# Modulations of two blocks side by side, norm sums in four column groups, modulations turned by transposes

## Chip, cores and metric

The kernel runs on one core of a Trainium2 chip. The metric is the device time of one execution in microseconds (us), lower is better; the time of a kernel is the median of several executions. The program computes in 32-bit floats, with nearly every large product split into a high and a low part.

## What is computed

One adaLN-modulated hybrid block (grouped-query attention beside a Fourier mixer) over 512 latent tokens of width 2048. The change touches only its first lines, and the head of the first projection:

```python
shift, scale, gate = jnp.split(silu_c @ w_ada[l] + b_ada[l], 3, axis=-1)
shift_c, scale_c, gate_c = jnp.split(silu_cc @ w_ada[l] + b_ada[l], 3, axis=-1)
h = _modulate(_rmsnorm(xs, norm_g[l]), shift[:, None], scale[:, None])   # h*(1+scale)+shift
p = h @ w_l            # attention, Fourier mixer, gates and output follow
```

The RMS norm needs the sum of squares of each token over all 2048 channels; the shift and the scale of each channel need a product of the vector `silu(c)` with 2048 rows of `w_ada`. Both must be there before the first block of 128 channels of `h` can enter a matmul.

## The kernel before, in words

Channels lie on the 128 partitions, so `xt` holds 16 blocks (`kb` 0 to 15) of 128 channels by 512 tokens. The part that the change touches is the start stage, about the first 150 us. It has three jobs on the matrix engine.

**Token norms** (`token_norms`, L513 to L536). ACT squares each block (L524, L528), DVE adds the squares of two blocks (L529, a 128x512 tile, 8 in all), and for each such tile one matmul with an all-ones stationary tile (L530) adds it over partitions into one PSUM bank, so that every partition has all 512 sums. Four ACT roots (L534) take 32 partitions each with the sums of 128 tokens, DVE takes the reciprocal (L535), and `spread` (L538) copies the result to all partitions through four matmuls (L541). The result scales every block.

**Modulations** (`modulate`, L559). For each block, `matvec` (L549) multiplies `c2` (32 columns, of which two are used: `c` and `c_ctx`) with 16 tiles of 128x256 of `w_ada`, on four groups of 32 columns of the array that work at the same time and write four groups of 32 PSUM rows (L553). ACT copies the result (`taken`, L569); `turned` (L571) multiplies it with `four`, a 0/1 matrix that adds the four groups and turns rows to columns in one step (L573, two matmuls with two columns each); DVE makes `gain` and `shift` of the block from them (L580, L582).

**Projection** (`start_work`, L638). As blocks of `h` come, they are multiplied with pieces of `w_in` of 1024 columns (L327 to L329 and L653 to L656): one step of `some(1)` is one 128x128 tile of the piece against 512 tokens, three matmuls (high by high, high by low, low by high), or, in pieces that pair two blocks in a private sum, six.

The order on PE is written by hand (`manual_schedule`), from L704 to L803: `modulate`, `columns` and `make_h` of each block stand between steps of the projection, so that the copy on ACT and the small DVE operations are covered by matmuls. From block six on, a loop (L766) takes one block after the other: three projection steps, the split of a weight piece on ACT and DVE (`split_next`, L176 and L177), `modulate`, one or two steps, `columns`, `make_h` (the high and low part of `h`, L611 to L614), and steps again. ACT and DVE have the same hand-written order up to block 13; for blocks 14 and 15 a scheduler orders them. The loads are issued by SP in the order of the program: for each block two loads of 1 MB of `w_ada` (`wada_load`, L481, tiles `wa`, four buffers, so the loads of a block wait until the block two before it has been multiplied) and one of 512 KB of `w_in` (`load_start`, tiles `wr`, four buffers).

After the start stage the rest of the program (Fourier mixer, the large projections, attention, output) follows; its order isn't touched.

Of the kernel before, what the change touches and what calls it, by code (L numbers as in the profile page):

```python
# [10 lines left out]
F32 = mybir.dt.float32  # L11
F32R = mybir.dt.float32r
ACT = mybir.ActivationFunctionType
ALU = mybir.AluOpType
# [105 lines left out]
def block_kernel(ctx, tc, xT, ctx_rows, ctx_toks, x, c_row, w_ss, w_gate, vecs, qkg, rope, dft_c, dft_s,  # L120
# [360 lines left out]
    def wada_load(kb):  # L481
        r = []
        for h in range(2):
            r.append(pap.tile([P, 8, 256], F32, tag="wada", bufs=4, name=uid("wa")))
            ask(nc.sync, r[-1], w_ss[kb, :, 8 * h : 8 * h + 8, :])
        return r

    for n in range(len(XCH)):
# [6 lines left out]

    c2 = pap.tile([P, KK, 32], F32, name="c2")
    nc.vector.memset(c2, 0.0)
    four = pap.tile([P, 2], F32, name="four")
    nc.vector.tensor_reduce(four, ident.rearrange("p (g r) -> p r g", g=4)[:, 0:2, :], axis=AX.X, op=ALU.add)
# [10 lines left out]
    fsq = [ppool.tile([P, 2, 2, T], F32R, name="fsq0")]  # L510
    rx = pap.tile([P, T], F32, name="rx")
    wacc = bank3()
    def token_norms():  # L513

        t = hm_tile([P, 2, T], F32, name=uid("nm"))
        pick, r = t[:, 0, :].rearrange("p (t c) -> p t c", t=4), t[:, 1, :P]
        nc.gpsimd.memset(pick, 0.0)
        for t in range(4):
            nc.gpsimd.memset(pick[32 * t : 32 * t + 1, t, :], 1.0)
        acc = bank2()  # L520
        for q in range(0, KK, 2):
            two = hm_tile([P, 2, T], F32, name=uid("sq"))
            a, b = two[:, 0, :], two[:, 1, :]
            nc.scalar.activation(a, xt[:, q, :], ACT.Square)  # L524
            if q in (6, 10):
                nc.vector.tensor_tensor(b, xt[:, q + 1, :], xt[:, q + 1, :], op=ALU.mult)
            else:
                nc.scalar.activation(b, xt[:, q + 1, :], ACT.Square)  # L528
            nc.vector.tensor_tensor(a, a, b, op=ALU.add)  # L529
            nc.tensor.matmul(acc, ones, a, start=q == 0, stop=q == KK - 2)  # L530

        for t in range(4):
            k = slice(32 * t, 32 * t + 32)
            nc.scalar.activation(r[k], acc[k, t * P : t * P + P], ACT.Sqrt, bias=eps_t[k, 0:1], scale=1.0 / D)  # L534
        nc.vector.reciprocal(r, r)  # L535
        return pick, r  # L536

    def spread(pick, r):  # L538
# [1 line left out]
        for t in range(4):  # L540
            nc.tensor.matmul(acc[:, t * P : t * P + P], pick[:, t, :], r, start=True, stop=True)  # L541
        return acc

    def warm(n, src):

        for _ in range(n):
            nc.tensor.matmul(wacc[:, :256], ones, src, start=True, stop=True)

    def matvec(kb, h):  # L549
        acc, w = two[kb][:, :256], wada[kb][h]  # L550
# [17 lines left out]
        wada.pop(kb)  # L568
        return nc.scalar.copy(o, two[kb][:, :256])  # L569

    def turned(sp, o):  # L571
        for i in range(2):
            nc.tensor.matmul(sp[:, 2 * i : 2 * i + 2], o[:, P * i : P * i + P], four, start=True, stop=True)  # L573

    def columns(kb):
        sp, o = two.pop(kb)[:, 256:], o_of.pop(kb)
        turned(sp, o)
        if kb == 0:
            warm(3, o)
        nc.vector.tensor_scalar(gain[:, kb, :], sp[:, 2:4], bsc1[:, kb : kb + 1], ng[:, kb : kb + 1],  # L580
                                op0=ALU.add, op1=ALU.mult)
        last = nc.vector.tensor_scalar(shift[:, kb, :], sp[:, 0:2], bada[:, kb : kb + 1], None, op0=ALU.add)  # L582
        return last

    rx0, y_of = [], {}
# [118 lines left out]
    with tc.manual_schedule(engines={E.PE}):  # L704
# [3 lines left out]
        rx0.append(spread(*norms))  # L708
        matvec(0, 1)
        with tc.manual_schedule(engines={E.Activation, E.DVE}):  # L710
            split_next()
            nc.scalar.copy(rx, rx0[0])
            by_root(0)
            taken(0)
            wada[2] = wada_load(2)
            load_start()
# [15 lines left out]
            some(2)  # L732
            for kb in range(1, 4):
                k = kb + 1
                some(2)
                by_root(k)
                modulate(k, split_next)
                if kb < 3:
                    wada[k + 2] = wada_load(k + 2)
                    load_start()  # L740
                hold()
                some(2)
                columns(k)
                row_hi(k)
                release()
# [20 lines left out]
            for kb in range(4, KK - 4, 2):  # L766
                some(3)
                split_next()
                for i in range(2):
                    k = kb + 2 + i  # L770
                    if i:
                        some(3)
                        split_next()
                    modulate(k)
                    if k + 2 < KK:
                        wada[k + 2] = wada_load(k + 2)
                        for _ in range(2 if k + 2 == KK - 3 else 1):
# [5 lines left out]
                    if k >= 8:  # L783
                        form_row(k - 8)
                some(1)
                if kb == KK - 6:
                    split_table(0)
                    split_from(get(("dftc", 0)), fch[:, 0, :], fch[:, 1, :])
                    load_start()
        for i in range(2):  # L790
            k = KK - 2 + i
            some(2)
            modulate(k)
            some(2 - i)
            columns(k)
            ins = make_h(k)
            with behind(ins):
                split_next()
                form_row(k - 8)
# [1166 lines left out]
```

## Time and profile before

| | |
|---|---|
| median of 3 runs | 1306.31 us (1306.24 to 1306.71) |
| the profiled execution | 1307.42 us |
| its span (first to last instruction) | 1305.7 us |
| PE busy | 1280.5 us, 98% of the span |
| DVE, ACT busy | 993.6 us, 687.5 us |
| the chain that ended last | PE 88%, DMA 4%, DVE 3%, ACT 2%, issue 2% |
| mean DMA rate over the first 140 us | 346 GB/s |

The profile is of one execution; times in it are us from the span's start. PE is the matrix engine, ACT the scalar engine, DVE the vector engine, SP the engine that issues most loads. A row of the timeline gives the start, the length, the engine, the source line, output<-inputs, the sizes, and how many instructions were merged into it. Matmuls are pipelined: what counts is the distance of the starts of two matmuls, not the length of one. A 32-bit matmul shows as two records ("passes"), so eight matmuls with c2 are 16 records.

### The profile page before, as it was taken

To read this page: it belongs to the slowest core of one execution; us is meant where nothing else is said; L and a number is where in the kernel's file an instruction comes from. 1 tells how busy PE (TensorE), PEld (TensorE's weight loads), DVE (VectorE), ACT (ScalarE), POOL (GpSimd) and SP (SyncE) were. 2 spreads that over 40 slices of the span, in tenths; PEclk is the share of its full clock that TensorE was granted. 3 is DMA by queue.
4 is the path that set the end of the run, shared out by engine and by line. 5 is a ranking of instruction groups with operands and counts; after the bars stand their busy time and mean duration, and the time that the engine had idled before them with its cause. 6 is when DMAs were issued, how large, how long until landed. Compare 5 with 4: busy or idle time off the path is not lost.

```text
span 1305.7 us, 17605 instructions
## 1 busy us (share of the span) xinstructions
PE 1280.5 (98%) x6554; PEld 1051.1 (81%) x6554; DVE 993.6 (76%) x1286; ACT 687.5 (53%) x1081; POOL 170.1 (13%) x220
## 2 busy tenths in 40 slices
PE   7999999999999999999999999999999999999997
PEld 3677888888888788888888888888888888888885
DVE  4656899979787787758677766688898767887676
ACT  5322655545556455444254554666667646464554
POOL 0000011110202111011021010011110212221210
PEclk9999999999999999999999999999999999999998
DMA  9988487888898889977869897467862899998985
GB/s 379 392 346 339 161 246 194 233 234 277 205 299 251 231 284 283 303 202 186 262 205 282 275 232 248 170 225 239 258 223 82 238 256 236 248 211 232 222 202 170
DMA packets 104053, 318.54 MB, mean 244 GB/s; under 512 B 9856, under 2 KB 33024, under 8 KB 99872
## 3 DMA queue, kind: packets, MB, share of 16 engines
q1 hardware_dynamic: 54912, 197.86, 41.7%
q0 software_dynamic: 26736, 97.14, 34.7%
q10 hardware_dynamic: 22320, 22.42, 5.0%
q8 instruction: 51, 0.84, 0.2%
q14 instruction: 34, 0.28, 0.1%
HBM read 283.30 MB, written 34.09 MB: 243 GB/s over the span
## 4 chain that ended last, share of the span: by engine, by line
PE 88%; DMA 4%; DVE 3%; ACT 2%; issue 2%; POOL 0%; SPq 0%; DVEq 0%; ACTq 0%; POOLq 0%
PE banks L327 9%; PE banks L328 9%; PE banks L329 9%; PE x L328 8%; PE x L329 8%; PE x L327 8%; PE y L329 7%; PE y L327 7%; PE y L328 7%; PE banks L1454 2%; PE pd L553 2%; DMA s<-yb_d 2%; PE pb L327 2%; PE pb L329 1%; PE pb L328 1%
## 5 line engine op out<-in xcount | busy, mean ns | idle before, releaser
L176 ACT ACTIVATE whi<-R 128x1024 fp32r<-128x1024 f32 x138 | 145.9, 1060 | 143.9 <-PE banks L329 49.2
L177 DVE TENSOR_TENSOR wlo<-R,whi 128x1024 fp32r<-128x1024 f32 x138 | 168.0, 1222 | 60.9 <-ACT whi L176 60.5
L177 DVE TENSOR_TENSOR wlo<-wr,whi 128x1024 fp32r<-128x1024 f32 (+1 forms) x122 | 147.3, 1213 | 61.2 <-ACT whi L176 60.9
L176 ACT ACTIVATE whi<-wr 128x1024 fp32r<-128x1024 f32 (+1 forms) x122 | 127.5, 1051 | 112.7 <-PE y L329 38.5
L327 PE MATMUL banks<-whi,s 128*128 128x512 f32 x396 | 157.0, 397 | 2.1 <-DVE ev L1021 1.5
L329 PE MATMUL banks<-whi,s 128*128 128x512 f32 x396 | 155.1, 392 | 0.0
L328 PE MATMUL banks<-wlo,s 128*128 128x512 f32 x396 | 155.0, 391 | 0.0
L328 PE MATMUL x<-wlo,s 128*128 128x512 f32 x356 | 138.7, 390 | 2.1 <-DVE wlo L177 2.1
L327 PE MATMUL x<-whi,s 128*128 128x512 f32 x356 | 138.8, 390 | 0.0
L329 PE MATMUL x<-whi,s 128*128 128x512 f32 x356 | 138.5, 389 | 0.0
L327 PE MATMUL y<-whi,s 128*128 128x512 f32 x308 | 120.1, 390 | 0.5 <-DVE cxe L1174 0.4
L329 PE MATMUL y<-whi,s 128*128 128x512 f32 x308 | 119.8, 389 | 0.5 <-DVE s L177 0.5
L328 PE MATMUL y<-wlo,s 128*128 128x512 f32 x308 | 119.9, 389 | 0.0
L280 POOL DMA_DIRECT2D R<-in_w_g x64 | 56.0, 874 | 415.9 <-DVE wlo L177 261.5
L176 ACT ACTIVATE s<-wr 128x512 fp32r<-128x512 f32 (+2 forms) x95 | 61.3, 677 | 66.8 <-DMA wr<-in_w_g 21.0
L177 DVE TENSOR_TENSOR s<-wr,s 128x512 fp32r<-128x512 f32 (+2 forms) x95 | 68.0, 749 | 27.6 <-ACT s L176 26.7
L327 PEld LDWEIGHTS banks<-whi,s 128*128 128x128 f32 x396 | 74.4, 188 | 17.6 <-ACT whi L176 1.9
L329 PEld LDWEIGHTS banks<-whi,s 128*128 128x128 f32 x396 | 74.4, 188 | 15.6
L328 PEld LDWEIGHTS banks<-wlo,s 128*128 128x128 f32 x396 | 74.4, 188 | 14.0 <-DVE wlo L177 0.2
L328 PEld LDWEIGHTS x<-wlo,s 128*128 128x128 f32 x356 | 66.8, 188 | 16.6 <-DVE wlo L177 2.9
L329 PEld LDWEIGHTS x<-whi,s 128*128 128x128 f32 x356 | 66.8, 188 | 13.9
L327 PEld LDWEIGHTS x<-whi,s 128*128 128x128 f32 x356 | 66.8, 188 | 13.7
(310 smaller groups left out, 2828.3 us busy)
## 6 DMA issues: line engine op xcount, KB each, us to landing
wr<-in_w_g SPq DMA_DIRECT2D x128, 512.0 KB, 5.4
wa<-in_w_ss SPq DMA_DIRECT2D x32, 1024.0 KB, 7.4
R<-in_w_g POOLq DMA_DIRECT2D x64, 512.0 KB, 7.3
R<-in_w_g SPq DMA_DIRECT2D x32, 512.0 KB, 5.9
wr<-in_w_gate SPq DMA_DIRECT2D x32, 512.0 KB, 4.8
wr<-in_w_o SPq DMA_DIRECT2D x24, 512.0 KB, 7.6
R<-in_w_o POOLq DMA_DIRECT2D x24, 512.0 KB, 8.8
wr<-in_w_pab SPq DMA_DIRECT2D x20, 512.0 KB, 6.1
```

The source lines that it names most:

```text
L176: first = nc.scalar.activation(hi, src, ACT.Copy)
L177: return first, nc.vector.tensor_tensor(lo, src, hi.bitcast(F32), op=ALU.subtract)
L280: nc.gpsimd.dma_start(chain[e.pc], e.nxt, accum_op=ALU.add)
L327: nc.tensor.matmul(o, ah, bh, start=start, stop=False, skip_group_check=cont)
L328: nc.tensor.matmul(o, ah, bl, start=False, stop=False, skip_group_check=cont)
L329: nc.tensor.matmul(o, al, bh, start=False, stop=stop, skip_group_check=cont)
L553: nc.tensor.matmul(acc[32 * j : 32 * j + 32], c2[:, n, :], w[:, k, :], start=n < 4, stop=n >= KK - 4)
L1454: nc.tensor.transpose(tp[:, k * P : (k + 1) * P], p[:, k * P : (k + 1) * P], ident)
```

## The change

Four edits, all in the start stage.

- **Norm sums.** Each pair tile of squares is now summed by four matmuls with 32 columns of ones each (L536): token group `t` of 128 tokens goes to PSUM rows `32t` to `32t+31`. So one ACT root over 128x128 takes the place of four (L540). Behind each of the first seven pairs two filler matmuls of 128x256 (`warm`, L516) are queued on PE, behind the last pair one; their output is not used.
- **Turned by transposes.** `turned` now transposes both halves of the copied result (L575, two transposes of 128x128), and `factors` adds the four groups by a DVE `tensor_reduce` (L586) before `gain` and `shift`.
- **Two blocks side by side.** From block six on, `modulate` of two blocks stands together, and so do their transposes; the projection steps between them are put elsewhere: eight ahead of the pair, one between the modulates and the transposes, three behind. For blocks 14 and 15 two steps stand ahead, one between, five behind.
- **Small ones.** The second `w_ada` load of block 0 is issued as two of 512 KB; in block 0 the split of the first weight piece is moved behind the copy of the norms; block 2's `modulate` is one step later.

```diff
     for q in range(0, KK, 2):
-            nc.tensor.matmul(acc, ones, a, start=q == 0, stop=q == KK - 2)
-
-        for t in range(4):
-            k = slice(32 * t, 32 * t + 32)
-            nc.scalar.activation(r[k], acc[k, t * P : t * P + P], ACT.Sqrt, bias=eps_t[k, 0:1], scale=1.0 / D)
+            for t in range(4):
+                nc.tensor.matmul(acc[32 * t : 32 * t + 32, :P], ones[:, :32], a[:, t * P : t * P + P],
+                                 start=q == 0, stop=q == KK - 2)
+            warm(2 if q < KK - 2 else 1, two[:, 0, :256])
+
+        nc.scalar.activation(r, acc[:, :P], ACT.Sqrt, bias=eps_t[:, 0:1], scale=1.0 / D)
         nc.vector.reciprocal(r, r)
...
-    def turned(sp, o):
+    def turned(kb):
+        o = o_of.pop(kb)
         for i in range(2):
-            nc.tensor.matmul(sp[:, 2 * i : 2 * i + 2], o[:, P * i : P * i + P], four, start=True, stop=True)
+            nc.tensor.transpose(two[kb][:, 256 + P * i : 256 + P * i + P], o[:, P * i : P * i + P], ident)
...
+    def factors(kb):
+        sp = two.pop(kb)[:, 256:]
+        r = pap.tile([P, 2, 2], F32, tag="ada_r", bufs=2, name=uid("adr"))
+        nc.vector.tensor_reduce(r, sp.rearrange("p (h g r) -> p h r g", h=2, g=4)[:, :, 0:2, :], axis=AX.X, op=ALU.add)
...
             for kb in range(4, KK - 4, 2):
                 some(3)
                 split_next()
+                some(5)
+                split_next()
+                k = kb + 2
                 for i in range(2):
-                    k = kb + 2 + i
-                    if i:
-                        some(3)
-                        split_next()
-                    modulate(k)
+                    modulate(k + i)
...
-                    some(2 - i)
-                    columns(k)
-                    make_h(k, lambda: some(i))
-                    some(i)
+                some(1)
+                for i in range(2):
+                    turned(k + i)
+                factors(k)
+                make_h(k, lambda: some(1))
+                factors(k + 1)
+                make_h(k + 1, lambda: some(1))
...
+        some(2)
+        k = KK - 2
         for i in range(2):
-            k = KK - 2 + i
-            some(2)
-            modulate(k)
-            some(2 - i)
-            columns(k)
-            ins = make_h(k)
+            modulate(k + i)
+        some(1)
+        for i in range(2):
+            turned(k + i)
+        for i in range(2):
+            factors(k + i)
+            ins = make_h(k + i)
             with behind(ins):
                 split_next()
-                form_row(k - 8)
+                form_row(k + i - 8)
             if not i:
                 load_start()
+        some(4)
         some(1)
         some(8)
```

Three places, as the built programs order them.

PE at the end of the norms, before: the last two pair tiles (`s_189`, `s_194`) into `pd_158`, the two halves of block 0's modulation with the spreading of the norms (`pc_213`) between them, and the turning.

```order
L530 MATMUL pd_158<-s_189,ones 128x512
L530 MATMUL pd_158<-s_194,ones 128x512
L553 MATMUL pd_204<-wa_121,c_135 32x256 x8
L541 MATMUL pc_213<-s_152 128x128 x4
L553 MATMUL pd_204<-wa_123,c_135 32x256 x8
L573 MATMUL pd_204<-four,ado_234 128x2 x2
```

The same place of the change (`s_218` and `s_228` are the last two pair tiles, `pc_148` takes the filler):

```order
L536 MATMUL pd_157<-s_218,ones 32x128 x4
L516 MATMUL pc_148<-s_218,ones 128x256 x2
L536 MATMUL pd_157<-s_228,ones 32x128 x4
L516 MATMUL pc_148<-s_228,ones 128x256
L554 MATMUL pd_239<-wa_121,c_136 32x256 x8
L547 MATMUL pc_248<-s_151 128x128 x4
L554 MATMUL pd_239<-wa_123,c_136 32x256 x8
L575 MATMUL pd_239<-ident,ado_269 128x128 x2
```

Each pair tile went from one matmul to four narrow ones and two of filler, and nothing else stands elsewhere.

PE at blocks 14 and 15, before (`pd_1134` is block 14, `pd_1184` block 15, `wa` their `w_ada` halves, `pb` the projection):

```order
L329 MATMUL pb_260<-s_1031,wlo_1050 128x512
L553 MATMUL pd_1134<-wa_1015,c_135 32x256 x8
L553 MATMUL pd_1134<-wa_1017,c_135 32x256 x8
L327 MATMUL pb_261<-s_1031,whi_1049 128x512
...
L329 MATMUL pb_262<-s_1031,wlo_1050 128x512
L573 MATMUL pd_1134<-four,ado_1151 128x2 x2
L327 MATMUL pb_259<-s_1031,whi_1049 128x512
...
L329 MATMUL pb_260<-s_1031,wlo_1050 128x512
L553 MATMUL pd_1184<-wa_1072,c_135 32x256 x8
L553 MATMUL pd_1184<-wa_1074,c_135 32x256 x8
```

The same place of the change (`pd_1197` is block 14, `pd_1216` block 15):

```order
L329 MATMUL pb_297<-s_1140,wlo_1071 128x512
L554 MATMUL pd_1197<-wa_1093,c_136 32x256 x8
L554 MATMUL pd_1197<-wa_1095,c_136 32x256 x8
L554 MATMUL pd_1216<-wa_1118,c_136 32x256 x8
L554 MATMUL pd_1216<-wa_1120,c_136 32x256 x8
L327 MATMUL pb_298<-s_1140,whi_1070 128x512
L328 MATMUL pb_298<-s_1141,whi_1070 128x512
L329 MATMUL pb_298<-s_1140,wlo_1071 128x512
L575 MATMUL pd_1197<-ident,ado_1214 128x128 x2
L575 MATMUL pd_1216<-ident,ado_1233 128x128 x2
```

Block 15's modulation moved ahead of twelve projection matmuls and of block 14's turning.

DVE at block 14, before: from `gain` of block 14 to the low part of the next weight piece (`wlo_1169`).

```order
L580 TENSOR_SCALAR gain<-pd_1134,bsc_98,small 128x2
L582 TENSOR_SCALAR shift<-pd_1134,small 128x2
L611 SCALAR_TENSOR_TENSOR xt<-xt,gain,rx 128x512
L614 SCALAR_TENSOR_TENSOR s_1164<-xt,shift,s_1163 128x512
L622 TENSOR_TENSOR d_1172<-shift 128x1
L623 TENSOR_TENSOR S_68<-xt 128x256
L177 TENSOR_TENSOR wlo_1169<-wr_1019,whi_1168 128x1024
```

The same stretch of the change (the piece is `wlo_1252` here):

```order
L586 TENSOR_REDUCE adr_1242<-pd_1197 128x4
L586 TENSOR_REDUCE adr_1261<-pd_1216 128x4
L587 TENSOR_SCALAR gain<-adr_1242,bsc_98,small 128x2
L589 TENSOR_SCALAR shift<-adr_1242,small 128x2
L618 SCALAR_TENSOR_TENSOR xt<-xt,gain,rx 128x512
L587 TENSOR_SCALAR gain<-adr_1261,bsc_98,small 128x2
L589 TENSOR_SCALAR shift<-adr_1261,small 128x2
L618 SCALAR_TENSOR_TENSOR xt<-xt,gain,rx 128x512
L621 SCALAR_TENSOR_TENSOR s_1247<-xt,shift,s_1246 128x512
L629 TENSOR_TENSOR d_1255<-shift 128x1
L630 TENSOR_TENSOR S_68<-xt 128x256
L177 TENSOR_TENSOR wlo_1252<-wr_1097,whi_1251 128x1024
```

Block 15's factors came ahead of block 14's low part and of the weight piece.

More of the change, by code (lines that the diff above doesn't have):

```diff
@@ L512, in block_kernel, with warm @@
     wacc = bank3()
+    def warm(n, src):
+        for _ in range(n):
+            nc.tensor.matmul(wacc[:, :256], ones, src, start=True, stop=True)
     def token_norms():
@@ L542, in spread @@
         return acc
-    def warm(n, src):
-        for _ in range(n):
-            nc.tensor.matmul(wacc[:, :256], ones, src, start=True, stop=True)
     def matvec(kb, h):
@@ L741, in block_kernel @@
                 hold()
-                some(2)
+                some(2 - (kb == 1))
                 columns(k)
```

31 lines of the change are left out of this document (16 added, 15 removed).

## Prediction, made blind

> **What bounds the kernel now.** I read the page first, then busy time by stage, then the timeline of PE in the start stage.
>
> ```profile
> PE 1280.5 (98%) x6554; PEld 1051.1 (81%) x6554; DVE 993.6 (76%) x1286; ACT 687.5 (53%) x1081; POOL 170.1 (13%) x220
> PE 88%; DMA 4%; DVE 3%; ACT 2%; issue 2%; POOL 0%; SPq 0%; DVEq 0%; ACTq 0%; POOLq 0%
> 0.00:24.30 24.30, 15.01 (x66) 6.97 (x66) 11.32 (x26) 14.73 (x27) 1.91 (x11) 1.00 0.94 367
> 24.30:135.00 110.70, 110.68 (x858) 78.92 (x858) 69.75 (x130) 33.44 (x50) 0.00 (x0) 1.00 0.89 350
> 135.00:1296.00 1161.00, 1154.53 (x5633) 965.26 (x5631) 909.21 (x1122) 636.46 (x998) 168.16 (x209) 1.00 0.81 232
> ```
>
> The rows by stage give length, then busy time of PE, PEld, DVE, ACT, POOL. PE is the bound: from 24.3 us on it idles 0.02 us up to 135, and 6.5 us in all the rest. So a microsecond taken off PE between 24 and 135 us is a microsecond of the whole, as long as nothing that PE waits for becomes late. Ahead of 24.3 PE is a link of a chain (squares, sums, root, reciprocal, spreading, modulation of block 0), and there only the chain counts. The change touches nothing after about 140 us.
>
> **Turning by transposes.** The first four rows are PE around one `turned` of before; the last four are existing transposes of 128x128 later in the kernel.
>
> ```profile
> 96.67 0.39 PE L329 MATMUL pb<-s,wlo 128*128 128x512 f32 x1
> 96.90 0.50 PE L573 MATMUL pd<-four,ado 128*128 128x2 f32 x4
> 97.26 0.48 PE L327 MATMUL pb<-s,whi 128*128 128x512 f32 x1
> 97.58 0.39 PE L328 MATMUL pb<-s,whi 128*128 128x512 f32 x1
> 828.39 0.39 PE L329 MATMUL banks<-whi,s 128*128 128x512 f32 x1
> 828.63 0.60 PE L1298 MATMUL banks<-ident,s 128*128 128x128 f32 x4
> 829.06 0.60 PE L1454 MATMUL banks<-ident,s 128*128 128x128 f32 x4
> 829.42 0.48 PE L327 MATMUL banks<-s,s 128*128 128x512 f32 x1
> ```
>
> From the start of one projection matmul to the start of the second behind the turning is 0.91 us; two ordinary steps of 0.23 off leave 0.45 for two matmuls, which are four passes: 0.11 a pass. Eight transposes last from 828.63 to 829.42, 0.79: 0.10 a transpose, and each is one pass: the row at 828.63 has four records for the four transposes that L1298 issues there, where L573 shows four records for two matmuls. With 0.11, two transposes cost 0.22 and save 0.22. In blocks 2 to 15 that is 14 x 0.22 = 3.1 us. In blocks 0 and 1 PE waits for ACT's high part, so the path runs over DVE: the transposes end 0.22 sooner, and the added reduction (the trace has none of this form; the nearest row is the `gain` from PSUM, 0.28 long, 0.20 until the next starts) takes that back. I take nothing there, with bounds of 0.2 either way for each.
>
> **Two blocks side by side.** The rows are one `modulate` between projection matmuls, and its last four records.
>
> ```profile
> 93.22 0.39 PE L329 MATMUL pb<-s,wlo 128*128 128x512 f32 x1
> 93.54 1.93 PE L553 MATMUL pd<-wa,c 128*32 128x256 f32 x32
> 95.08 0.40 PE L553 MATMUL pd<-wa,c 128*32 128x256 f32 x4
> 95.41 0.50 PE L327 MATMUL pb<-s,whi 128*128 128x512 f32 x1
> 95.74 0.40 PE L328 MATMUL pb<-s,whi 128*128 128x512 f32 x1
> ```
>
> 32 passes run as eight rounds of four groups: (95.08 - 93.54)/7 = 0.22 a round. The way in costs 0.32 where a step is 0.23, the last round 0.33 until the next matmul where a round is 0.22, and that matmul 0.33 again. So one `modulate` costs 95.74 - 93.22 - 0.46 = 2.06; a second one behind it adds eight rounds, 1.76. A pair saves 0.30, five pairs 1.5 us. The Trainium skill, TensorEngine Tiling, section Key Properties, says that a change of the tiling mode drains TensorE. The 0.32 and 0.33 agree with it; the same rule speaks against the next edit.
>
> **Norm sums.** DVE's first and last sum, then PE's passes slow and fast, the last, and the chain behind.
>
> ```profile
> 6.40 0.69 DVE L529 TENSOR_TENSOR s<-s 128x512 f32<-128x512 f32 x1 [2.80 <-ACT s L528]
> 15.15 0.69 DVE L529 TENSOR_TENSOR s<-s 128x512 f32<-128x512 f32 x1 [0.35 <-ACT s L528]
> 8.16 3.62 PE L530 MATMUL pd<-s,ones 128*128 128x512 f32 x4
> 12.77 2.31 PE L530 MATMUL pd<-s,ones 128*128 128x512 f32 x5
> 16.43 0.59 PE L530 MATMUL pd<-s,ones 128*128 128x512 f32 x1
> 16.95 1.07 PE L553 MATMUL pd<-wa,c 128*32 128x256 f32 x16
> 17.06 1.48 ACT L534 ACTIVATE s<-pd,eps_t 32x128 f32<-32x128 f32 x4 [1.94 <-PE pd L530]
> 18.57 0.95 DVE L535 RECIPROCAL s<-s 128x128 f32<-128x128 f32 x1 [2.73 <-ACT s L534]
> 19.67 1.13 PE L541 MATMUL pc<-s 128*128 128x128 f32 x8 [1.65 <-DVE s L535]
> 22.76 1.54 PE L547 MATMUL pc<-ado,ones 128*128 128x256 f32 x6
> ```
>
> A pass of 512 columns first takes (3.62 - 1.06)/3 = 0.85 and later (2.31 - 0.59)/4 = 0.43; the doubling comes at about 12.2 us. Pairs come from DVE every (15.15 - 6.40)/7 = 1.25 us. Before, PE needs two fast passes, 0.86, for a pair, has caught up by the sixth pair, and ends 1.2 us behind the last sum, at 17.0.
>
> After, a pair is eight narrow passes and four of filler, and the narrow ones are not seen in this form. Two rounds of half the columns: 0.14 (estimate: half of 0.22 and a little). Round to first filler 0.22 (0.33 less the shorter round). Four fillers of (1.54 - 0.38)/5 = 0.23, 0.93. Back to narrow 0.09. Sum 1.4 us fast, 2.7 slow: **longer than the 1.25 between arrivals**, so the filler, not DVE, sets the pace. From 7.15: first pair to 9.85, the second almost done at 12.2, ended at 12.4; five more to 19.4; the last pair's rounds end at 19.85. That is 2.8 later than 17.0. Then it gets shorter: one root of 0.36 for four (1.48), the reciprocal 0.95 and the ways between give 21.4; on PE one filler pair and block 0's half modulation, which before ran beside the roots, also end at 21.4. Before it was 19.67. **I take +1.7.** Bounds: if a switch costs nothing, a pair is 1.08, PE keeps up from the fourth pair on its way to 17.7, and the spreading starts at 19.2, -0.5; with 0.2 more in each pair it is +3.
>
> The Trainium skill, TensorE: Matmul & The Clock Gate, Part 1, says that the doubling follows a free-running window of about 3.4 us, so its moment varies. No row here shows a second moment. By that rule executions would spread, and each us that it comes later costs half a us here.
>
> **What the pair does to loads and DVE at the end.** In the middle of the stage a pair follows the one before after 15.2 us (3.6 for the pair, 0.45 for transposes, 48 steps of 0.23 and two short ways). The loads that a pair asks for are read off two requests of before:
>
> ```profile
> 109.57 0.42 PE L553 MATMUL pd<-wa,c 128*32 128x256 f32 x4
> 110.70 1.19 SPq L465 DMA_DIRECT2D wa<-in_w_ss  x2
> 116.68 1.19 SPq L465 DMA_DIRECT2D wa<-in_w_ss  x2
> wa<-in_w_ss SPq DMA_DIRECT2D x1, 1024.0 KB, 6.9
> ```
>
> The first `wa` is asked 1.1 us after its modulation starts; the fourth, asked at about 117.5 (the second issue of the row at 116.68), lands 6.9 later, at 124.4 (the fourth row is that one issue): 13.7 after the first request, with an issue waiting in the queue all the time. So, P being the start of a pair, the last half of the next lands at P + 14.8. In the middle it is needed at P + 15.2 + 2.6: 3 us to spare. But the last pair comes sooner: 3.6 for the pair, 1.5 for six matmuls, 0.45 for transposes, 4.2 and 1.4 for 24 matmuls, 0.1: P + 11.1, and its last half is needed twelve rounds later, at P + 13.7. PE then waits 1.1 to 1.4; **+1.3.** SP has nothing queued behind that is needed sooner. Bounds: 0 (a load 1.1 faster) and 2.
>
> Second, DVE at block 14.
>
> ```profile
> 128.27 0.50 PE L573 MATMUL pd<-four,ado 128*128 128x2 f32 x4
> 128.88 0.28 DVE L580 TENSOR_SCALAR gain<-pd,bsc,small 128x2 f32<-128x2 f32 x1 [3.02 <-PE pd L573]
> 129.08 0.21 DVE L582 TENSOR_SCALAR shift<-pd,small 128x2 f32<-128x2 f32 x1
> 129.21 0.75 DVE L611 SCALAR_TENSOR_TENSOR xt<-xt,gain,rx 128x512 f32<-128x512 f32 x1
> 130.74 0.75 DVE L614 SCALAR_TENSOR_TENSOR s<-xt,shift,s 128x512 fp32r<-128x512 f32 x1 [0.79 <-ACT s L612]
> 131.41 0.15 DVE L622 TENSOR_TENSOR d<-shift 128x1 f32<-128x1 f32 x1
> 131.48 0.42 DVE L623 TENSOR_TENSOR S<-xt 128x256 f32<-128x256 f32 x1
> 131.82 1.22 DVE L177 TENSOR_TENSOR wlo<-wr,whi 128x1024 fp32r<-128x1024 f32 x1
> ```
>
> By the distances of these starts, from the first transpose: 0.5 to the first reduction, 0.4 for two, 0.33 and 0.67 for block 14's factors and product, 0.33 and 0.67 for block 15's, 0.67 for the low part, 0.41, and 1.22: `wlo` is there at 5.2. PE comes to the third matmul of that piece after 0.4 for transposes and 17 steps, at 4.3. Before, one block's factors fewer stood ahead of it on DVE, and one modulation more on PE. So PE now waits, **+0.9** (bounds 0 and 1.3). In the loop the low parts come 1 us ahead of PE by the same sums, so nothing is added there; if that cover went, each pair would pay what is missing. The split `w_ada` load and block 2's later step cost nothing: block 0's second half stands behind the spreading of the norms, which is later than before, and PE has other steps for block 2.
>
> **The sum.** -3.1 - 1.5 + 1.7 + 1.3 + 0.9 = -0.7 us on the profiled 1307.42, so 1306.7; the median of the runs shown is 1.1 lower, 1306.31, and 0.7 off it is 1305.6.
>
> **Rivals.** (a) The forecast, all five terms: 1305.6, by its bounds 1303.8 to 1308; chance 0.57.
> (b) PE keeps up with the norm sums: -0.5 in place of +1.7, 1303.4. For it: the narrow form is unseen. Against: the 0.32 and 0.33 of each switch. 0.15.
> (c) The waits at the end don't come, because the last load or `wlo` is sooner: -4.6 + 1.7, 1303.4. 0.11; (b) and (c) both: 1301.2, 0.03.
> (d) Slower: the doubling of PE's pace comes late, since narrow passes with a fill of mixed kinds keep the array less busy than 512-column passes. Each us later is +0.5; it decides from 18.8 us on (+3.3), and with no doubling in the whole stage the sums end near 26, +6, 1311.5. For it: the first five us of PE are slow at full load already. Against: the filler alone is two thirds of the time. 0.08.
> (e) The change doesn't do what it says: transposes run as two passes of 128 columns and save nothing. 1306.31 - 1.5 + 3.9 = 1308.7; against it stands the row at 828.63. 0.06.
>
> **How the numbers follow.** About 0.2%, 2.6 us, is what can be told from no change here: below 1303.7 is faster, above 1308.9 slower. (b), (c) and both lie just below the line: 0.29, of which 0.05 fall back within, 0.24 faster. (d) and half of (e) and the far end of (a) give 0.13 slower. The rest, 0.63, is the same. The range 1303.0 to 1308.2 holds (a) nearly whole, (b) and (c), and leaves out the double gain and (d).
>
> **What would show it.** Right: L536 records with PE busy without a gap from 7 to 21 us, the root starting near 19.9; a pair of modulations 3.8 us in place of 4.1; two records for each turning; PE idle over 1 us before L554 at block 15 (waiting for `wa`) and about 0.9 before L329 on `wlo` a few us later. Wrong: a root before 18 us (b), no waits in the last pair (c), passes still 0.85 apart at 15 us (d).

## The result, and the profile after

The changed kernel takes 1308.32 us (median of 14 runs, 1306.63 to 1314.32), the kernel before 1307.49 us in the same runs (14 runs, 1304.83 to 1311.86). The ratio is 1.0005, 95% interval 0.9994 to 1.0016: no difference that can be measured. The forecast was 0.7 us less, within 0.2%, so the outcome is as forecast (against the 1306.31 that the forecast started from, the ratio gives 1307.0). An outcome of no difference says little of the sum behind it: the times of either kernel scatter by 7 us, and the sum is tested in the traces.

The profiled execution of the changed kernel has a span of 1305.7 us, as before. PE's busy time, from its page (before it was 1280.5):

```profile
PE 1278.5 (98%) x6600; PEld 1051.8 (81%) x6600; DVE 995.2 (76%) x1301; ACT 683.6 (52%) x1078; POOL 167.5 (13%) x220
```

PE works 2 us less and the span is the same, so PE waits 2 us more. The busy time by stage (length, then busy time of PE, PEld, DVE, ACT, POOL), from the first projection on, says where:

```profile
25.95:135.00 109.05, 106.23 (x827) 75.81 (x828) 71.68 (x146) 35.26 (x52) 0.00 (x0) 1.00 0.89 349
135.00:1296.00 1161.00, 1153.75 (x5631) 965.59 (x5631) 908.80 (x1122) 631.90 (x996) 165.60 (x209) 1.00 0.82 232
```

The first projection comes at 25.95 where it came at 24.32, and from there to 135 us PE idles 2.82 us where it idled 0.02. From 135 us on the two traces hardly differ. A good mark for what the stage gained or lost is the first matmul of the Fourier step, which takes the stage's result; here it is in the timeline of PE:

```profile
150.28 0.28 PE L327 MATMUL pb<-fch,uh 128*128 128x256 f32 x1
```

Before, it started at 150.37. The change wins 0.09 us up to there, where 0.7 were forecast. The timeline of PE (start, length, engine, line, output<-inputs, form, count), with the root of ACT, shows the norm sums (rows between are left out):

```profile
7.01 0.66 PE L536 MATMUL pd<-s,ones 128*32 128x128 f32 x8 [7.01 <-DVE s L534]
9.60 0.65 PE L536 MATMUL pd<-s,ones 128*32 128x128 f32 x8
16.40 0.43 PE L536 MATMUL pd<-s,ones 128*32 128x128 f32 x8
17.82 0.43 PE L536 MATMUL pd<-s,ones 128*32 128x128 f32 x8
19.24 0.42 PE L536 MATMUL pd<-s,ones 128*32 128x128 f32 x8
19.73 0.37 ACT L540 ACTIVATE s<-pd,eps_t 128x128 f32<-128x128 f32 x1 [4.59 <-PE pd L536]
21.23 1.15 PE L547 MATMUL pc<-s 128*128 128x128 f32 x8
25.95 0.50 PE L660 MATMUL pb<-s,whi 128*128 128x512 f32 x1 [0.34 <-ACT s L605]
```

From the sums of one pair to those of the next are 17.82 - 16.40 = 1.42 us fast and 9.60 - 7.01 = 2.6 slow; DVE's last sum was done at 15.9, but PE reaches it at 19.24, and the root starts at 19.73 where before the four roots started at 17.06.

The middle of the stage, a pair of modulations and its transposes (three matmuls between the fourth row and the fifth are left out, and one between the last two):

```profile
80.60 0.39 PE L329 MATMUL pb<-s,wlo 128*128 128x512 f32 x1
80.92 3.66 PE L554 MATMUL pd<-wa,c 128*32 128x256 f32 x64
84.51 0.50 PE L327 MATMUL pc<-s,whi 128*128 128x512 f32 x1
84.85 0.40 PE L328 MATMUL pc<-s,whi 128*128 128x512 f32 x1
85.78 0.39 PE L329 MATMUL pc<-s,wlo 128*128 128x512 f32 x1
86.00 0.60 PE L575 MATMUL pd<-ident,ado 128*128 128x128 f32 x4
86.68 0.39 PE L328 MATMUL pc<-s,whi 128*128 128x512 f32 x1
```

The pair costs 84.85 - 80.60 - 0.46 = 3.79 us, against twice 2.06. Two turnings are four records, and cost 86.68 - 85.78 - 0.46 = 0.44, against twice 0.45.

And the last pair, with what PE waited for in brackets, then (behind rows that are left out) the matmul that waits for `wlo`:

```profile
122.33 1.93 PE L554 MATMUL pd<-wa,c 128*32 128x256 f32 x32
124.94 1.07 PE L554 MATMUL pd<-wa,c 128*32 128x256 f32 x16 [0.67 <-DVE part L643]
127.33 1.07 PE L554 MATMUL pd<-wa,c 128*32 128x256 f32 x16 [1.32 <-DMA wa<-in_w_ss]
128.33 0.50 PE L327 MATMUL pb<-s,whi 128*128 128x512 f32 x1
133.25 0.39 PE L328 MATMUL pb<-s,whi 128*128 128x512 f32 x1
134.24 0.50 PE L329 MATMUL pb<-s,wlo 128*128 128x512 f32 x1 [0.60 <-DVE wlo L177]
134.58 0.40 PE L327 MATMUL pb<-s,whi 128*128 128x512 f32 x1
```

From the pair to the next matmul are 6.00 us, against 84.51 - 80.92 = 3.59 in the middle of the stage: 2.41 lost, where 1.3 was forecast and 2 was the bound. At `wlo` 134.24 - 133.25 - 0.23 = 0.76 are lost, and 0.11 more at the next step. The timeline puts the first of these waits down to DVE; DVE and the third half of `wa` end within 0.1 us of each other there. The run with another order of loads, below, shows that it is the load.

### The profile page after: what moved, and what is told of

Read it like the earlier page. It is cut to its first block, busy times and chain, and to the rows that moved or that the text cites. A ratio compares the mean times of both kernels' runs of the same rounds, so it can differ in the third digit from the quotient of the medians.

```text
span 1305.7 us, 17712 instructions
## 1 busy us (share of the span) xinstructions
PE 1278.5 (98%) x6600; PEld 1051.8 (81%) x6600; DVE 995.2 (76%) x1301; ACT 683.6 (52%) x1078; POOL 167.5 (13%) x220
## 4 chain that ended last, share of the span: by engine, by line
PE 84%; DMA 5%; DVE 5%; issue 4%; ACT 2%; POOL 0%; ACTq 0%; DVEq 0%; SPq 0%; POOLq 0%
PE banks L327 10%; PE banks L329 9%; PE banks L328 9%; PE x L328 7%; PE x L329 7%; PE x L327 7%; PE y L329 6%; PE y L327 6%; PE y L328 6%; PE pd L554 2%; PE banks L1468 2%; DMA wr<-in_w_g 2%; PE pb L327 1%; PE pb L329 1%; PE pb L328 1%
## 5 line engine op out<-in xcount | busy, mean ns | idle before, releaser
L329 PEld LDWEIGHTS banks<-whi,s 128*128 128x128 f32 x396 | 74.4, 188 | 15.5
L328 PEld LDWEIGHTS x<-wlo,s 128*128 128x128 f32 x356 | 66.8, 188 | 15.7 <-DVE wlo L177 1.9
```

The costliest lines, as they stand in the source:

```text
L328: nc.tensor.matmul(o, ah, bl, start=False, stop=False, skip_group_check=cont)
L329: nc.tensor.matmul(o, al, bh, start=False, stop=stop, skip_group_check=cont)
```

## Experiments

Four marks are compared: the root's start, the first projection, the first Fourier matmul, and the distance of the last two. The moment at which PE's pace doubles is the start of the trace's record of a full clock.

| run | pace doubles | root | first projection | Fourier | distance |
|---|---|---|---|---|---|
| before | 12.24 | 17.06 | 24.32 | 150.37 | 126.05 |
| before, again (b2) | 11.37 | 17.04 | 24.29 | 150.41 | 126.12 |
| after | 12.06 | 19.73 | 25.95 | 150.28 | 124.33 |
| after, again (a2) | 10.65 | 19.09 | 25.31 | 151.08 | 125.77 |
| wide | 12.42 | 16.87 | 24.17 | 147.98 | 123.81 |
| f1 | 13.65 | 17.38 | 23.59 | 148.22 | 124.63 |
| f0 | 21.66 | 16.92 | 24.93 | 150.46 | 125.53 |
| fn | 11.66 | 18.74 | 24.94 | 148.44 | 123.50 |
| tail | 10.54 | 19.09 | 25.32 | 146.69 | 121.37 |
| queue | 11.91 | 19.65 | 25.86 | 148.96 | 123.10 |
| late2 | 11.96 | 19.86 | 26.08 | 150.33 | 124.25 |
| single | 11.46 | 17.01 | 24.31 | 147.32 | 123.01 |
| wt | 12.94 | 17.16 | 24.46 | 145.85 | 121.39 |
| best | 11.55 | 17.75 | 23.95 | 145.98 | 122.03 |

The runs from wide to late2 were each timed once: wide 1300.82, f1 1303.35, f0 1306.91 and fn 1308.61 us beside 1305.32 for the kernel before, and tail 1305.59, queue 1308.76 and late2 1310.02 beside 1310.54. Single times say little where those of one kernel spread over 7 us, so these runs are read by their marks.

**The norm sums of before under the rest of the change (wide).**

```diff
-            for t in range(4):
-                nc.tensor.matmul(acc[32 * t : 32 * t + 32, :P], ones[:, :32], a[:, t * P : t * P + P],
-                                 start=q == 0, stop=q == KK - 2)
-            warm(2 if q < KK - 2 else 1, two[:, 0, :256])
+            nc.tensor.matmul(acc, ones, a, start=q == 0, stop=q == KK - 2)
...
-        nc.scalar.activation(r, acc[:, :P], ACT.Sqrt, bias=eps_t[:, 0:1], scale=1.0 / D)
+        for t in range(4):
+            k = slice(32 * t, 32 * t + 32)
+            nc.scalar.activation(r[k], acc[k, t * P : t * P + P], ACT.Sqrt, bias=eps_t[k, 0:1], scale=1.0 / D)
```

> The changed kernel with the norm sums of before (passes of 512 columns, four roots) and all the rest of the change. Theory: all of the 1.63 us by which the first projection came later (25.95 against 24.32) is the norm sums, and the transposes with their added reduction are worth nothing in block 0: the spreading starts at 19.7, the first projection at 24.3, the Fourier step at 148.65 (150.28 less 1.63). Rival: part of the 1.63 is the reduction or the later split in block 0: the first projection at 24.6 or later.

The first projection comes at 24.17. The theory holds: all of the 1.63 us is the norm sums, and block 0's transposes and reduction cost nothing.

**Half the filler (f1).**

```diff
-            warm(2 if q < KK - 2 else 1, two[:, 0, :256])
+            warm(1 if q < KK - 2 else 1, two[:, 0, :256])
```

> The changed kernel with half the filler behind each pair of squares (two passes of 256 columns in place of four). Theory: filler and narrow passes set the pace, since a pair takes PE 1.42 us where the sums come every 1.25. Half the filler takes 0.43 off: 0.98 fast (1.7 slow), PE catches up with DVE at about the sixth pair, the sums end near 16.4 in place of 19.6, the root starts near 16.5 (19.73), the first projection comes near 22.9 (25.95) and the first matmul of the Fourier step near 147.3 (150.28). Rival 1, DVE and ACT set the pace: root unchanged at 19.7. Rival 2, the pace of PE does not double at about 12 us with less to do: the root near 18 and passes still 0.43 us per 256 columns at 15 us.

Its pairs, in the timeline of PE:

```profile
10.67 0.66 PE L536 MATMUL pd<-s,ones 128*32 128x128 f32 x8
12.41 0.66 PE L536 MATMUL pd<-s,ones 128*32 128x128 f32 x8
13.93 0.43 PE L536 MATMUL pd<-s,ones 128*32 128x128 f32 x8
14.91 0.43 PE L536 MATMUL pd<-s,ones 128*32 128x128 f32 x8
```

A pair is 1.74 slow and 0.98 fast as expected, so PE sets the pace; rival 1 falls. But the doubling came at 13.65, 1.6 us later than in the changed kernel, so the root starts at 17.38 and not at 16.5, and the first projection comes at 23.59 and not at 22.9 (still 0.73 earlier than in the kernel before). Rival 2 is right in part: the doubling was late, though by 15 us it had come.

**No filler (f0).** The line with `warm` is left out.

> The changed kernel with no filler behind the pairs. Theory of the pace: sums end 0.5 us behind the last sum of DVE, near 16.3, the root at 16.4. What then follows tells what the filler is for. If the clock doubles by itself or by the little that is left (0.23 to 0.45 us of PE in 1.25), the first projection comes near 22.8 and the Fourier step near 147.2. If it needs PE kept busy, the eight rounds of block 0 run at 0.43 us a round in place of 0.22 and the first projection matmuls at 0.46 in place of 0.23, until it doubles; at some 3 to 5 us of that the first projection comes near 23.5 and the Fourier step 2 to 3 us later than in the other case, near 149.5.

The root starts at 16.92. The doubling then comes only at 21.66, and the rounds of block 0 and the spreading run at half pace:

```profile
17.09 1.93 PE L553 MATMUL pd<-wa,c 128*32 128x256 f32 x16 [0.23 <-DMA wa<-in_w_ss]
18.95 2.08 PE L546 MATMUL pc<-s 128*128 128x128 f32 x8
```

The half modulation takes 1.93 us where it took 1.07 in the kernel before, the spreading 2.08 where it took 1.13. The first projection comes at 24.93, 0.6 later than before the change: this is what the filler is for. (At 127 us this execution also ran 3.41 us at half clock, told under a2.)

**Filler of the same length in the narrow form (fn).**

```diff
-            warm(2 if q < KK - 2 else 1, two[:, 0, :256])
+            for _ in range(4 if q < KK - 2 else 2):
+                for t in range(4):
+                    nc.tensor.matmul(wacc[32 * t : 32 * t + 32, :P], ones[:, :32], two[:, 0, t * P : t * P + P],
+                                     start=True, stop=True)
```

> The changed kernel with filler of the same length in the narrow form: eight rounds of 128 columns in four column groups (0.11 each, 0.9 us) in place of four passes of 256 columns (0.86 us), so that PE never changes its tiling between the pairs. Theory: of the 1.42 us of a pair, 0.23 are the sums, 0.86 the filler and the remaining 0.33 the two changes of tiling. Then a pair takes 1.13, less than 1.25, PE gains on DVE, and the sums end near 17.7 and the root starts near 17.8. Rival: the changes cost nothing and the filler alone is too long: the root stays near 19.7.

```profile
12.66 0.39 PE L536 MATMUL pd<-s,ones 128*32 128x128 f32 x8
13.75 0.39 PE L536 MATMUL pd<-s,ones 128*32 128x128 f32 x8
```

A pair takes 1.09 us: the two changes of tiling are the 0.33 that make the difference to 1.42, and without them PE gains on DVE. The Trainium skill, TensorEngine Tiling (Array Packing), section Key Properties, has the rule that a change of mode drains TensorE; it gives no price, and this run has one. The root starts 1 us later than expected, since PE stood still for 1.0 us at 15.7 us behind nothing that the profile shows.

**Blocks 14 and 15 one at a time (tail).** The last pair is written as in the kernel before, with the transposes.

> The changed kernel with blocks 14 and 15 one at a time as in the kernel before (two projection steps, modulation, two or one more steps, transposes, factors), pairs only for blocks 6 to 13. Theory: PE's two waits in the last pair (2.4 us for the halves of wa, 0.9 for the low part wlo) come because the pair asks for all four halves 4 us sooner and puts two blocks' factors ahead of wlo. Both waits go, and a pair's saving of 0.42 (0.32 for the ways in and out, 0.10 for the transposes of two blocks together) is given back: the Fourier step starts near 147.4 in place of 150.28. Rival: the loads of the last blocks are late by bandwidth and PE waits as long in block 15: the Fourier step near 149.8.

Block 15's modulation runs without a break, and neither it nor the step on `wlo` waits:

```profile
126.73 1.93 PE L554 MATMUL pd<-wa,c 128*32 128x256 f32 x32
```

The distance from the first projection to the Fourier step is 121.37, 2.96 less; 2.9 were expected. The Fourier step is still earlier than 147.4 because the doubling came 1.5 us sooner in this execution and with it the first projection by 0.63.

**The piece's load behind both blocks' (queue).**

```diff
                 for i in range(2):
                     modulate(k + i)
-                    if k + 2 + i < KK:
-                        wada[k + 2 + i] = wada_load(k + 2 + i)
-                        for _ in range(2 if k + 2 + i == KK - 3 else 1):
-                            load_start()
+                    wada[k + 2 + i] = wada_load(k + 2 + i)
+                for _ in range(3 if kb == KK - 8 else 2):
+                    load_start()
```

> The changed kernel with the 512 KB load of the next piece asked behind both wa of a pair, no longer between them. Theory: in the last pair that load lands 1.24 us ahead of the third half of wa and stands in its way on a DMA that moves over 400 GB/s throughout, so the third half lands near 123.6 and the fourth near 126.0 (124.8 and 127.3), the waits for wa go from 2.4 to about 1.1 us, and the Fourier step starts near 149.0. Rival: transfers in flight share the bandwidth whatever their order, so nothing moves: third and fourth half near 124.8 and 127.3, the Fourier step at 150.3.

SP's requests in the changed kernel, and then single issues with the time from issue to landing (the third half asked at 114.15, the fourth at 114.97):

```profile
112.38 1.19 SPq L465 DMA_DIRECT2D wa<-in_w_ss  x2
113.62 0.42 SPq L212 DMA_DIRECT2D wr<-in_w_start  x1
114.15 1.15 SPq L465 DMA_DIRECT2D wa<-in_w_ss  x2
```

```profile
wa<-in_w_ss SPq DMA_DIRECT2D x1, 1024.0 KB, 10.7
wa<-in_w_ss SPq DMA_DIRECT2D x1, 1024.0 KB, 12.3
```

They land at 124.8 and 127.3. In the other order, all four requests in a row, the time to landing of the third and the fourth (asked at 113.98 and 114.85), and the last pair on PE:

```profile
112.26 2.92 SPq L465 DMA_DIRECT2D wa<-in_w_ss  x4
```

```profile
wa<-in_w_ss SPq DMA_DIRECT2D x1, 1024.0 KB, 9.5
wa<-in_w_ss SPq DMA_DIRECT2D x1, 1024.0 KB, 11.2
```

```profile
122.21 2.80 PE L554 MATMUL pd<-wa,c 128*32 128x256 f32 x48
126.04 1.07 PE L554 MATMUL pd<-wa,c 128*32 128x256 f32 x16 [1.03 <-DMA wa<-in_w_ss]
```

They land at 123.5 and 126.0, the third half is no longer waited for, the pair takes 4.83 in place of 6.00, and the distance falls by 1.23 us. So moving the load of 512 KB that stood between those of the two blocks takes half of the wait away, and the first wait was one for the load too: DVE's `part` starts at 124.10 here, when PE already runs past that point. That load stood between the two blocks in the kernel before as well, so it isn't what the forecast missed; what that was is told below.

**DVE's work behind `wlo` (late2).**

```diff
-        for i in range(2):
-            factors(k + i)
-            ins = make_h(k + i)
-            with behind(ins):
-                split_next()
-                form_row(k + i - 8)
-            if not i:
-                load_start()
+        factors(k)
+        ins = make_h(k)
+        with behind(ins):
+            split_next()
+        load_start()
+        with behind(split_of[-1]):
+            factors(k + 1)
+            ins = make_h(k + 1)
+        with behind(ins):
+            form_row(k - 8)
+            split_next()
+            form_row(k - 7)
```

> The changed kernel with block 15's factors and product, and the two rows formed from blocks 6 and 7, put behind the low part wlo of the next piece on DVE. The prediction's step: wlo is late because 1.4 us more of DVE's work stands ahead of it; then the wait of PE for it (0.92 us over a step) goes and the Fourier step starts near 149.4. Rival: wlo can't start before ACT has made the high part whi, which stands behind block 14's high row on ACT and ends at 132.7, 0.27 us before wlo starts; then only 0.27 is won, and the Fourier step starts near 150.0.

The rows of ACT and DVE ahead of `wlo`, then that of PE at `wlo`:

```profile
131.07 0.72 ACT L619 ACTIVATE s<-xt,shift 128x512 fp32r<-128x512 f32 x1 [2.04 <-DVE xt L618]
131.70 1.04 ACT L176 ACTIVATE whi<-wr 128x1024 fp32r<-128x1024 f32 x1
```

```profile
131.83 0.75 DVE L621 SCALAR_TENSOR_TENSOR s<-xt,shift,s 128x512 fp32r<-128x512 f32 x1 [0.79 <-ACT s L619]
132.78 1.23 DVE L177 TENSOR_TENSOR wlo<-wr,whi 128x1024 fp32r<-128x1024 f32 x1 [0.20 <-ACT whi L176]
```

```profile
134.06 0.50 PE L329 MATMUL pb<-s,wlo 128*128 128x512 f32 x1 [0.29 <-DVE wlo L177]
```

The rival is right. With 1.4 us of DVE's work out of the way, DVE idles 0.20 for `whi`, which ACT makes behind block 14's high row, and PE still waits 0.29 (0.60). Then block 15's rows come late in turn: its low row ends on DVE at 136.75, and the matmuls there lose 0.2. The distance falls by 0.08 us in all.

**The transposes alone, the transposes with four pairs, and a narrow filler (single, wt, best)**, each timed against the kernel before on the same chip (1308.43 us, 13 runs). `single` is wide with all blocks one at a time, so the kernel before with turning by transposes and all of the change's small edits (the split load, the later split in block 0, block 2's later step). `wt` is wide with blocks 14 and 15 one at a time. `best` has fn's filler with `range(3 if q < KK - 2 else 0)`, and blocks 14 and 15 one at a time.

> The kernel before with its modulations turned by transposes, and nothing else of the change but the split first load. Theory: 14 blocks at 0.22 us: from the first projection to the Fourier step 126.05 - 3.1 = 122.95 us, the Fourier step near 147.2, 1.7 behind the kernel with four pairs (4 x 0.42), a ratio near 0.9976. Rival: the transposes save nothing since they are two passes each or their reduction on DVE is waited for: 126 us, ratio 1.000.

> The changed kernel with the norm sums of before and blocks 14 and 15 one at a time: the transposes and the four pairs of blocks 6 to 13 are left of the change. Theory: 24.2 to the first projection, then 121.4: the Fourier step near 145.6, 4.8 us ahead of the kernel before (150.37), and all of it reaches the end: a ratio near 0.9964. Rival: the lead is spent on waits further on (the low part wlo near 427 us, the R near 915 us), and the time is the same within 0.2%.

> The changed kernel with filler in the narrow form at three quarters of its length (six rounds of 128 columns behind each pair but the last) and blocks 14 and 15 one at a time. Theory: a pair takes 0.23 + 0.66 = 0.89 us fast and 1.8 slow, less than the 1.25 of DVE, so the sums end within half a us of DVE's last sum, near 16.3, the root starts near 16.4, and the first projection comes near 22.6; from there to the Fourier step 121.4 as in the run with single blocks at the end: Fourier near 144.0, 6.4 us ahead of the kernel before, a ratio near 0.995. Rival 1: the first blocks' loads are then late, PE waits for wa or the first pieces between 20 and 40 us, and the Fourier step comes near 145.5. Rival 2: with only 72% of PE's time filled after the doubling, the clock falls back to half for 3.4 us, and 1.7 us are lost.

| run | median us (runs) | ratio to before, 95% interval | Fourier step against before |
|---|---|---|---|
| single | 1301.94 (5) | 0.9950, 0.9938 to 0.9962 | -3.05 |
| wt | 1301.02 (6) | 0.9943, 0.9931 to 0.9956 | -4.52 |
| best | 1301.86 (8) | 0.9957, 0.9942 to 0.9971 | -4.39 |

`single` gives the transposes with the small edits: 126.05 - 123.01 = 3.04 us, 0.22 for each of 14 blocks. One turning in its trace costs 0.22 where it cost 0.45, so the small edits are worth about nothing. Its rival falls. `wt` beside it gives four pairs: 123.01 - 121.39 = 1.62, 0.4 each. `best` misses its start: PE stood still for 1.24 us at 16 us, and the first projection comes at 23.95 in place of 22.6. Neither of its rivals was the reason; it is the stall of fn once more, in the other kernel with many narrow matmuls. In both traces a packet of 16 KB of the instruction queue, 1 us long, starts 1.3 to 1.4 us ahead of the stall (14.3 and 14.7 us), and no other run has one before 20.9 us; whether PE stood still for instructions isn't shown. So `wt`, with two of the change's three parts and one place undone, is at least as good as any, and 0.6% faster than the kernel before, which the changed kernel isn't.

The three timed gains are larger than the stage gives: 6.5, 7.4 and 6.6 us against 3.05, 4.52 and 4.39. The surplus lies behind the Fourier step, where the programs are the same.

**Both kernels once more (b2, a2).**

> The kernel before once more, unchanged, for its profile: what differs between executions of one kernel. Theory: up to the Fourier step executions agree but for the moment of the doubling (Fourier step at 150.4, within 0.5 us), and the time differs by waits further on: for the low part wlo near 427 us (0 to 2 us), for R near 915 us (0.2 to 3 us), and by 1.7 us for each stretch of 3.41 us at half clock that such a wait brings. Rival: the stage itself differs by some us from one execution to the next, and a step of 1 us in it can't be read from one profile each.

> The changed kernel once more, unchanged. Theory: waits of 2.4 us for wa and 0.9 us for wlo in the last pair again, a pair of narrow and filler passes 1.42 us again, the first projection at 25.95 moved by 0.42 us for each us by which the doubling comes before or after 12.06, and the Fourier step at 150.3 moved by as much. Rival: the waits in the last pair are an accident of one execution and differ by more than half a us.

The stage of the kernel before repeats to 0.04 us. Behind it, its two executions differ: the one shown before waits 1.9 us for a `wlo` at 427 us, this one 2.9, and then runs 3.41 us at half clock. The waits there in `wt` and `single` are 0.5 and 0.7. In the wide run there is none. That is where executions scatter; whether a stage that ends sooner makes it better there stays open, with one profile each.

In a2 the waits of the last pair are there again, 0.55 and 1.34 us, and behind the second PE runs at half clock. The timeline of PE, then the stretches ahead of the half clock and in it (length, then PE's busy time; the granted clock is the third number from the end):

```profile
126.58 1.86 PE L554 MATMUL pd<-wa,c 128*32 128x256 f32 x16 [1.34 <-DMA wa<-in_w_ss]
```

```profile
123.30:126.71 3.41, 1.51 (x28) 0.63 (x24) 2.41 (x4) 0.37 (x1) 0.00 (x0) 1.00 0.87 335
```

```profile
126.72:130.10 3.38, 3.38 (x21) 1.78 (x16) 0.00 (x0) 0.37 (x1) 0.00 (x0) 0.50 0.79 298
```

The distance is 125.77 in place of 124.33: the half clock took 1.4 us more than the waits themselves. f0 has the same at the same place. Of the eight executions with a pair at the end, two lost this, and six did not.

## Why the forecast was right, and where it was wrong

| step | forecast | measured | from |
|---|---|---|---|
| turning, blocks 2 to 15 | -3.1 | -3.04 | single |
| pairs, five | -1.5 | -2.0 | wt against single, 0.4 each |
| norm sums | +1.7 | +1.63 | first projection; wide |
| `wa` in the last pair | +1.3 | +2.41 | 6.00 against 3.59 |
| `wlo` | +0.9 | +0.87 | rows at 133.25 to 134.58 |
| blocks 0 and 1 | 0 | +0.1 | block 1, 5.38 against 5.29 |
| sum | -0.7 | -0.03 (Fourier step: -0.09) | |

**Turning** held as priced, and rival (e), two passes a transpose, falls: two records a turning, 0.11 us apart.

**Pairs** were under-priced by 0.1 each. The ways in and out are 2 x 2.06 - 3.79 = 0.33; where the rest lies wasn't followed. The five in the table are four measured ones (wt) and a fifth at the same price.

**Norm sums**: the mechanism and its size held, 1.42 a pair against 1.4, the root at 19.73 against 19.85, the spreading at 21.23 against 21.4. fn shows that it takes the changes of tiling to put a pair above the 1.25 of DVE, and f1 that half the filler brings it below as well; rival (b) needed a free change of tiling. Rival (d), a doubling that comes late, did not come true with the full filler: 10.5 to 12.1 in the five executions that have it. Its price was about right (0.5 a us): tail and after differ by 1.52 us in the doubling and by 0.64 in the root, 0.42 a us. By the Trainium skill, TensorE: Matmul & The Clock Gate, Part 1, the window runs freely and the moment varies by plus or minus 0.5 us; here the moments lie 1.5 us apart with the same filler.

**`wa` in the last pair** is the term that was mis-sized. The pair does begin at P + 11.1 (P, the start of the pair before, is 111.25), as forecast (the parts as written there add up to 11.25). But the time of the fourth half, P + 14.8, was carried over from the kernel before as first request plus 13.7, and here it is 14.9 (112.38 to 127.28): the fourth half lands at P + 16.0, and even the third comes 0.6 late. The 512 KB load that queue moves isn't the difference. The kernel before asked for it in the same place, between the halves at 110.70 and 116.68, and its time is in the 13.7:

```profile
111.94 0.42 SPq L212 DMA_DIRECT2D wr<-in_w_start  x1
```

The 1.2 us are lost between the landings of the first and the second half: 2.51 us lie between them in the kernel before (115.67 to 118.17), 3.66 in the changed one (117.41 to 121.07). What the DMA queues moved in these two stretches, before and after (packets, MB, share of 16 engines):

```profile
q1 hardware_dynamic: 184, 1.02, 97.9%
```

```profile
q1 hardware_dynamic: 278, 1.52, 100.1%
q8 instruction: 1, 0.02, 1.7%
```

In the longer stretch half a MB of the loads asked later moves already, and a packet of the instruction queue (q8), 16 KB and about 1 us long, lies in it. From the first request for these five loads to their last landing it is 14.5 to 15.5 us in the eleven executions in which such a packet runs in that time. In before and b2 it runs outside, in fn it starts 0.3 us ahead of the end, and there it is 13.7, 13.7 and 14.2. fn asks in the same order and as close together as the changed kernel; its third half isn't waited for, and its fourth for 1.34, as forecast. So the packet is the likely cause, but no edit tested it. The forecast had no term for it. queue has the packet too, and wins about as much in another way. In addition, the forecast had no price for the half clock that may follow (a2).

**`wlo`** came out at 0.87 with a reason that was half wrong. The sum over DVE's instructions gave the right moment (5.2 forecast, 134.19 - 129.13 = 5.06 seen), but DVE is only one of two limits that lie 0.27 us apart: ACT's `whi` ends at 132.70, so that moving DVE's work is worth 0.3 there and 0.1 in all. Rival (c), that the waits at the end don't come, falls with after and a2.

So the sum was right to 0.6 us in part by luck: a gain under-priced by 0.5 stood against a wait under-priced by 1.1. Nothing of it reached the time: -0.1 us up to the Fourier step, and 0.7 us worse in a2 against b2.

## What to carry to other kernels

Work put side by side asks for its inputs sooner and in one burst: list each load in the queue between those that the pair needs, its own order included (moving one of 512 KB was worth 1.23 us here), take a landing time from more than one trace, and leave the last pair apart where nothing else is left to cover a load. A filler that keeps the clock up has to fit into the gap that it fills, with the price of its changes of tiling, or it becomes the pace. A PE wait of 1.3 to 2 us can cost as much again if it leaves a window of the clock half empty.

## What the runs showed of the hardware

**The clock's window.** Every stretch at half clock inside the five executions that had one (f0, a2, fn, late2, b2) is 3.41 us long. The stretch of 3.41 us ahead of it had PE busy for 0.51 to 1.65 us. Stretches on the same grid (a whole number of 3.41 us behind the doubling) that were busier kept the full clock: 1.69 us in tail and 1.78 in before (both near 425 us), 1.84 in after at its last pair. The limit is about half, but not sharp in the trace's busy time: in late2 a stretch with 1.61 kept the full clock, and one with 1.65 at 428 us didn't. In the other direction it takes more: with PE busy 3.04 of 3.41 us the pace did not double (f1), with 3.31 it did (tail). The Trainium skill, TensorE: Matmul & The Clock Gate, Part 1, gives 3413 ns for the window, which agrees, and an idle window as the condition for the fall; here a half-empty one was enough.

```profile
124.60:128.01 3.41, 1.61 (x28) 0.86 (x32) 1.92 (x3) 0.32 (x1) 0.00 (x0) 1.00 0.88 305
```

```profile
6.83:10.24 3.41, 3.04 (x20) 1.41 (x20) 2.22 (x4) 2.66 (x5) 0.00 (x0) 1.00 1.02 417
```

```profile
7.13:10.54 3.41, 3.31 (x21) 1.72 (x21) 2.11 (x5) 2.50 (x6) 0.00 (x0) 1.00 1.02 418
```

The first row is late2 at its last pair, the second f1, the third tail.

**A change of tiling** between matmuls of 128x128 and column groups, there and back, costs 0.33 us (fn against after).
